# Seven products instead of eight in every second step of a down projection

## The chip, the cores and the metric

The kernel runs on one core of a Trainium2 chip. The metric is the device time of one execution in microseconds: the median of three runs of the kernel before is 1230.73 us (1230.72 to 1230.82). Times inside an execution come from one profiled execution, which took 1231.12 us; its instructions span 1229.3 us of it.

A core has a matrix engine (TensorE, PE in the profile; its weight loads are PEld), a vector engine (VectorE, DVE), a scalar engine (ScalarE, ACT), a third elementwise engine (GpSimd, POOL) and a queue that issues transfers from memory (SyncE, SP). Each takes its instructions strictly in the order written for it and waits where an operand is not ready. Matrix products are written to PSUM, which has eight banks of 128 rows by 512 float32 columns; everything else works from SBUF.

## What is computed

A decoder layer over 272 tokens (16 learned ones and 256 of the input) of width 2048: a normalisation, one input projection, eight retention heads and four mLSTM heads, an output projection, and then a gated MLP of width 5632 with a causal convolution of three taps. Only the 256 input tokens leave. The part that matters here is the last line of the layer and the final normalisation:

```python
up = causal_dwconv(u @ w_up.astype(u.dtype), ffn_conv_w, ffn_conv_b)
gate, val = jnp.split(up, [FFN_DIM], axis=-1)
return h + (jax.nn.silu(gate) * val) @ w_down.astype(h.dtype)
...
h = rmsnorm(h, norm_final)
```

`silu(gate) * val` is a 256 x 5632 matrix, `w_down` is 5632 x 2048; the product of the two is "the down projection".

## The kernel before

**Split operands.** Every float32 operand of a large product is split into two parts of a narrower format that the matrix engine takes at full rate: `hi` is a rounded copy, made by ScalarE (`nc.scalar.copy`), and `lo = x - hi`, made by VectorE (`nc.vector.tensor_tensor` with both inputs in SBUF). A product is three matmuls: hi by hi, lo of the activations by hi of the weights, hi of the activations by lo of the weights. Weights arrive by a transfer of 512 KB (128 x 1024 float32) into a tile `wraw` (4 buffers), are split into `whi` and `wlo` (5 buffers each), and are used once; `load_w` (line 122) does this.

**Stages.** Input projection and heads, output projection, and then the MLP in two halves of 2816 hidden columns each (`for half in range(2)`). A half has an up projection (22 chunks `jj` of 128 hidden columns, gate and value; convolution and silu on VectorE and ScalarE; the result, split, goes to `mh` and `ml`), and a down projection over these 22 chunks. In the profiled execution the two down projections run from 720.5 to 843.7 us and from 1097.8 us to the end.

**The down projection.** For each of four column blocks `b` of 512 columns, two banks `pss` (one per half of the tokens, `tt`) collect the sum over 11 steps `q`. A step takes one weight tile of 2 x 128 hidden rows by 512 columns, and `product` issues six matmuls of 512 columns per token half: 12 a step, 132 a block, 528 a half. After a block, `add` puts the banks onto the residual `hn` (VectorE, one input in PSUM). In the second half `squares` (ScalarE) and `times_gain` (GpSimd) prepare the final normalisation. In the very last block the second token half lags four steps behind the first, so that the first half's normalisation and stores run under the second's products.

**Order.** The program is written straight; the framework that builds it places each instruction on its engine's queue by its own estimate of time, with the order of the text as priority. Tiles with a given number of buffers are reused in turn: the first writer of a new tile waits for the last reader of the tile that had its buffer.

Of the kernel before, what the change touches and what calls it, by code (L numbers as in the profile page):

```python
# [10 lines left out]
F32 = mybir.dt.float32  # L11
# [5 lines left out]
P = 128  # L17
# [66 lines left out]
def trunk(ctx: ExitStack, tc: tile.TileContext, io, out: bass.AP):  # L84
# [75 lines left out]
    def rsqrt_m2(work, v, n, after):  # L160

        r0 = work.tile([P, T], F32, name="r0", bufs=1)
# [3 lines left out]
        t = work.tile([P, T], F32, name="rt", bufs=1)  # L166
# [41 lines left out]
    with pool("sq", 1, side="right") as sqp:  # L208
# [51 lines left out]
        with tc.high_priority():  # L260
# [4 lines left out]
            r = rsqrt_m2(wk, ms[:, :T], T, squared)  # L265
# [119 lines left out]
    def variance(s2, mean):  # L385
# [8 lines left out]
        return rsqrt_m2(wk, var[:, :NQ], NQ, copied)  # L394
# [177 lines left out]
    ssq = up.tile([P, NQ], F32, name="ssq")  # L572

    def out_tile(n, ps):
# [5 lines left out]
        if n == 0:  # L580
            nc.scalar.activation(ssq, h, AF.Square)
        else:
            s2 = wk2.tile([P, NQ], F32, name="s2b")
            sq = nc.scalar.activation(s2, h, AF.Square)
            nc.gpsimd.tensor_tensor(out=ssq, in0=ssq, in1=s2, op=ALU.add)
            return sq
# [11 lines left out]

    mixp_cm.__exit__(None, None, None)

    def norm2():
        ms2 = at.tile([P, 512], F32, name="atps")
        nc.tensor.matmul(ms2[:, :NQ], inv_dm, ssq, start=True, stop=True)
        r = rsqrt_m2(wk2, ms2[:, :NQ], NQ, squared)
# [6 lines left out]
    gfin = midp.tile([P, DM], F32, name="gfin")  # L611
    nc.gpsimd.dma_start(gfin, io["gfin"])
    ss4 = midp.tile([P, 2, 5], F32, name="ss4")
    junk = midp.tile([P, 512], F32, name="junk")
# [65 lines left out]

    NQD = NHF // 2
    for half in range(2):
        mh = midp.tile([P, NHF, SEQ], F32R, name="mh")
        ml = midp.tile([P, NHF, SEQ], F32R, name="ml")
        for jj in range(NHF):
# [10 lines left out]
            copied = nc.scalar.copy(mh[:, jj, :], gt)  # L696
            parted = nc.vector.tensor_tensor(out=ml[:, jj, :], in0=gt, in1=mh[:, jj, :].bitcast(F32), op=ALU.subtract)
# [5 lines left out]

        def product(ps, tt, q, w, first=0, last=NQD - 1, c0=0):

            hi, lo = w
            rows = slice(tt * P, (tt + 1) * P)
            cols = slice(c0, c0 + ps.shape[1])
            for i in range(2):
                k = 2 * q + i  # L710
                nc.tensor.matmul(ps, mh[:, k, rows], hi[:, i, cols], start=k == 2 * first, stop=False)  # L711
                nc.tensor.matmul(ps, ml[:, k, rows], hi[:, i, cols], start=False, stop=False)  # L712
            for i in range(2):
                k = 2 * q + i
                nc.tensor.matmul(ps, mh[:, k, rows], lo[:, i, cols], start=False, stop=k == 2 * last + 1)  # L715
# [5 lines left out]
        if half == 1:  # L721
            wk2_cm.__exit__(None, None, None)
            up_cm.__exit__(None, None, None)
            more_cm = pool("more", 4, side="right")
            more = more_cm.__enter__()
        for b in range(4):
            pss = [at.tile([P, 512], F32, name="atps") for _ in range(2)]
            last = half == 1 and b == 3


            lag = 4 if last else 0
            c = b * 512
            ws = {}
            for q in range(NQD):
                ws[q] = load_w(io["wd"][b, half * NQD + q], [P, 2, 512], more if last and q % 2 else wpool)
                product(pss[0], 0, q, ws[q])
                if q >= lag:
                    product(pss[1], 1, q - lag, ws.pop(q - lag), last=NQD - 1 - lag)
            if not last:
                for tt in range(2):  # L740
                    add(pss[tt], tt, c)
                    if half == 1:
                        squares(tt, b, c, c + 512)
                        times_gain(tt, c, c + 512)
                continue
            add(pss[0], 0, c)
# [3 lines left out]
            add(pss[1], 1, c)  # L750
            for i in range(2):
                ps = at.tile([P, 512], F32, name="atps")[:, 0:256]
                for q in sorted(ws):
                    product(ps, 1, q, ws[q], NQD - lag, c0=i * 256)
                add(ps, 1, c + i * 256)
# [89 lines left out]
```

## Time and profile before

| what | value |
|---|---|
| median of three runs | 1230.73 us |
| the profiled execution | 1231.12 us |
| span of its instructions | 1229.3 us |
| TensorE busy | 1219.7 us, 99% of the span |
| VectorE busy | 841.0 us, 68% |
| ScalarE busy | 655.9 us, 53% |
| GpSimd busy | 53.2 us, 4% |
| weights and inputs read | 222.98 MB, 185 GB/s over the span |

A row of a group has the line of the program, the engine, the operation, the output and the inputs, the shape and the count, and then the busy time of all and the mean of one in ns. A row of a timeline has the start in us, the duration in us, the engine, the line and the operation; "x2" means that two instructions in a row were merged into one row. "Idle before" names what ended a wait. Matmuls overlap in a pipeline, so that what one costs is the distance from its start to the next one's and not its duration.

### The profile page before, as it was taken

What the parts mean: (1) busy time and instruction counts of PE and PEld (TensorE: products, weight loads), DVE (VectorE), ACT (ScalarE), POOL (GpSimd) and SP (SyncE); (2) the same over time, 40 slices, a digit from 0 to 9 for tenths busy, and PEclk for the clock granted to TensorE, in tenths of its full rate; (3) what the DMA queues carried; (4) which work ended last, traced back from release to release, by engine and by line L of the source; (5) the groups of instructions that cost most, each with busy time, mean ns of one, the idle gap of its engine ahead of it and who ended that gap; (6) DMA issues with size and microseconds to landing.
All of it is one profiled execution on the core that took longest, in us unless ns stands there. A gap on an engine that the chain in (4) does not pass through costs nothing.

```text
span 1229.3 us, 22301 instructions
## 1 busy us (share of the span) xinstructions
PE 1219.7 (99%) x9034; PEld 1169.6 (95%) x9034; DVE 841.0 (68%) x1267; ACT 655.9 (53%) x879; POOL 53.2 (4%) x63
## 2 busy tenths in 40 slices
PE   9999999999999999999999999999999999999997
PEld 9999999999999999999999988889999999998886
DVE  8967878767775767787887754445677677664452
ACT  8747656656557556555555543334555555554441
POOL 0100001111100110000000000000000000000000
PEclk9999999999999999999999999999999999999999
DMA  7765565565564656555555665655555556556561
GB/s 275 275 205 159 176 190 172 185 190 175 178 189 143 216 180 216 177 186 187 176 186 188 175 185 189 188 188 189 184 178 188 185 178 187 181 180 188 188 206 69
DMA packets 73287, 228.88 MB, mean 186 GB/s; under 512 B 13408, under 2 KB 17632, under 8 KB 73056
## 3 DMA queue, kind: packets, MB, share of 16 engines
q1 hardware_dynamic: 71952, 223.85, 57.7%
q0 software_dynamic: 656, 2.76, 0.7%
q8 instruction: 70, 1.15, 0.4%
q10 hardware_dynamic: 576, 0.85, 0.2%
q14 instruction: 33, 0.27, 0.1%
HBM read 222.98 MB, written 4.46 MB: 185 GB/s over the span
## 4 chain that ended last, share of the span: by engine, by line
PE 99%; DMA 0%; ACT 0%; DVE 0%; SPq 0%; DVEq 0%; issue 0%; ACTq 0%
PE mmps L137 25%; PE mmps L140 25%; PE mmps L138 25%; PE atps L711 7%; PE atps L712 7%; PE atps L715 7%; PE atps L380 1%; PE atps L372 0%; DMA hT<-in_xT 0%; PE atps L137 0%; PE atps L140 0%; PE atps L381 0%; PE atps L138 0%; PE atps L373 0%; PE atps L382 0%; PE atps L238 0%
## 5 line engine op out<-in xcount | busy, mean ns | idle before, releaser
L128 ACT CAST whi<-wraw 128x1024 fp32r<-128x1024 f32 x404 | 423.2, 1050 | 474.4 <-PE mmps L138 254.8
L130 DVE TENSOR_TENSOR wlo<-wraw,whi 128x1024 fp32r<-128x1024 f32 x404 | 495.8, 1229 | 186.0 <-ACT whi L128 181.0
L138 PE MATMUL mmps<-ul,whi 128*128 128x258 f32 x1408 | 345.8, 283 | 0.0
L137 PE MATMUL mmps<-uh,whi 128*128 128x258 f32 x1408 | 345.5, 282 | 0.0
L137 PEld LDWEIGHTS mmps<-uh,whi 128*128 128x128 f32 x1408 | 266.1, 189 | 0.1
L138 PEld LDWEIGHTS mmps<-ul,whi 128*128 128x128 f32 x1408 | 265.1, 188 | 0.1
L137 PE MATMUL mmps<-xh,whi 128*128 128x272 f32 (+2 forms) x864 | 220.1, 287 | 0.0
L138 PE MATMUL mmps<-xl,whi 128*128 128x272 f32 (+2 forms) x864 | 218.9, 286 | 0.0
L140 PE MATMUL mmps<-uh,wlo 128*128 128x258 f32 x1408 | 198.9, 284 | 0.0
L140 PEld LDWEIGHTS mmps<-uh,wlo 128*128 128x128 f32 x1408 | 182.4, 189 | 0.0
L137 PEld LDWEIGHTS mmps<-xh,whi 128*128 128x128 f32 x864 | 162.8, 188 | 0.1
L138 PEld LDWEIGHTS mmps<-xl,whi 128*128 128x128 f32 x864 | 162.5, 188 | 0.0
L711 PE MATMUL atps<-whi,mh 128*128 128x512 f32 (+1 forms) x360 | 140.5, 391 | 0.0
L712 PE MATMUL atps<-whi,ml 128*128 128x512 f32 (+1 forms) x360 | 140.2, 390 | 0.0
L140 PE MATMUL mmps<-xh,wlo 128*128 128x272 f32 (+2 forms) x864 | 127.1, 286 | 0.0
L140 PEld LDWEIGHTS mmps<-xh,wlo 128*128 128x128 f32 x864 | 114.7, 188 | 0.0
L715 PE MATMUL atps<-wlo,mh 128*128 128x512 f32 (+1 forms) x360 | 110.7, 388 | 0.0
L625 DVE TENSOR_TENSOR cu<-mmps,rstd 128x258 f32<-128x258 f32 x88 | 37.6, 427 | 97.6 <-PE mmps L140 97.1
L711 PEld LDWEIGHTS atps<-whi,mh 128*128 128x128 f32 x360 | 67.6, 188 | 15.8
L715 PEld LDWEIGHTS atps<-wlo,mh 128*128 128x128 f32 x360 | 67.0, 188 | 16.0
L712 PEld LDWEIGHTS atps<-whi,ml 128*128 128x128 f32 x360 | 67.6, 188 | 15.1
L138 PE MATMUL mmps<-mixl,whi 128*128 128x258 f32 x256 | 63.1, 283 | 0.0
(213 smaller groups left out, 1040.3 us busy)
## 6 DMA issues: line engine op xcount, KB each, us to landing
wraw<-in_wu SPq DMA_DIRECT2D x176, 512.0 KB, 3.5
wraw<-in_wi SPq DMA_DIRECT2D x108, 512.0 KB, 4.0
wraw<-in_wd SPq DMA_DIRECT2D x88, 512.0 KB, 3.5
wraw<-in_wo SPq DMA_DIRECT2D x32, 512.0 KB, 3.7
wraw<-in_w SPq DMA_DIRECT2D x7, 320.0 KB, 5.1
hT<-in_xT SPq DMA_DIRECT2D x7, 272.0 KB, 5.5
e<-in_decay POOLq DMA_DIRECT2D x8, 209.0 KB, 3.0
away<-turns SPq DMA_DIRECT2D x4, 288.0 KB, 4.4
```

What stands on the lines that cost most here:

```text
L128: nc.scalar.copy(hi, raw)
L130: nc.vector.tensor_tensor(out=lo, in0=raw, in1=hi.bitcast(F32), op=ALU.subtract)
L137: nc.tensor.matmul(ps, hi[:, k, :], xh(kk), start=kk == first, stop=False)
L138: nc.tensor.matmul(ps, hi[:, k, :], xl(kk), start=False, stop=False)
L140: nc.tensor.matmul(ps, lo[:, k, :], xh(kk), start=False, stop=kk == last)
L380: nc.tensor.matmul(ps[:, 0:NQ], lhs(0), pT[:, 0:CA], start=True, stop=False)
L625: nc.vector.tensor_tensor(out=u, in0=ps[:, :NQ], in1=rstd2, op=ALU.mult)
L711: nc.tensor.matmul(ps, mh[:, k, rows], hi[:, i, cols], start=k == 2 * first, stop=False)
L712: nc.tensor.matmul(ps, ml[:, k, rows], hi[:, i, cols], start=False, stop=False)
L715: nc.tensor.matmul(ps, mh[:, k, rows], lo[:, i, cols], start=False, stop=k == 2 * last + 1)
```

## The change

The 11 steps of a half are divided into six plain ones (q = 0, 2, 4, 6, 8, 10) and five fast ones (1, 3, 5, 7, 9), and two neighbouring column blocks are done at once, so that a step covers 2 token halves x 2 chunks of hidden rows x 2 column blocks. A plain step is what it was, for two weight tiles: 24 matmuls. A fast step takes the 2 x 2 block product by the Strassen-Winograd scheme: seven products of three matmuls, 21 in all, of sums of blocks.

- **Sums of the activations** (four 128 x 128 sums for each pair of chunks, S1 to S4) are made in the up projection by GpSimd in the tile `tb`, and split into `sh` and `sl`, which hold seven operands per fast step in place of four.
- **Sums of the weights** are made in each fast step: the two tiles `raw0` (a `wraw`) and `raw1` (a tile of its own, one buffer) arrive; GpSimd makes four sums of 128 x 512 into `ta` and `tb` (one buffer each), one after the other; then `raw0`, one half of `raw1`, `ta` and `tb` are split by ScalarE and VectorE and multiplied.
- **Banks.** Four banks `cs` collect the four results as before; three of the seven products go straight into them. The other four products collect over the five fast steps in the four banks `ps`, and `share` then distributes them over the four results: a copy on ScalarE and eight additions on VectorE, through the tile `ta`.
- **The end.** In the second half the pair of blocks 2 and 3 does its plain steps for block 2 alone (12 matmuls each); block 3's six plain steps follow behind, with the old lag between the token halves.
- **Room.** To make room, the work tiles of the second normalisation and of the squares move to other tiles, `gfin` (the final gain, 1 MB) is loaded only once the last up projection is over, and the pool `more` of the last block has 3 buffers in place of 4.

```diff
-        mh = midp.tile([P, NHF, SEQ], F32R, name="mh")
-        ml = midp.tile([P, NHF, SEQ], F32R, name="ml")
+        mh = midp.tile([P, 2 * len(PLAIN), SEQ], F32R, name="mh")
+        ml = midp.tile([P, 2 * len(PLAIN), SEQ], F32R, name="ml")
+        sh = midp.tile([P, len(FAST), 7, P], F32R, name="sh")
+        sl = midp.tile([P, len(FAST), 7, P], F32R, name="sl")
...
+                nc.gpsimd.tensor_tensor(out=sums[:, S1, :], in0=a21, in1=a22, op=ALU.add)
+                nc.gpsimd.tensor_tensor(out=sums[:, S3, :], in0=a11, in1=a21, op=ALU.subtract)
+                nc.gpsimd.tensor_tensor(out=sums[:, S2, :], in0=sums[:, S1, :], in1=a11, op=ALU.subtract)
+                nc.gpsimd.tensor_tensor(out=sums[:, S4, :], in0=a12, in1=sums[:, S2, :], op=ALU.subtract)
+                split(sh[:, f, A12:, :], sl[:, f, A12:, :], gt.rearrange("p (a t) -> p a t", a=2))
+                copied, parted = split(sh[:, f, 0:4, :], sl[:, f, 0:4, :], sums)
...
+        def seven(w0, w1, q, cs, ps, fresh):
+
+            f = FAST.index(q)
+            raw0 = wpool.tile([P, 2, 512], F32, name="wraw", bufs=4)
+            nc.sync.dma_start(raw0, w0)
+            raw1 = midp.tile([P, 2, 512], F32, name="raw1")
+            nc.sync.dma_start(raw1, w1)
+
+            ta, tb = (midp.tile([P, 2, 512], F32, name=n) for n in ("ta", "tb"))
+            sums = ((ta, 1, raw1[:, 1, :], raw1[:, 0, :], ALU.subtract), (tb, 0, ta[:, 1, :], raw0[:, 0, :], ALU.add),
+                    (ta, 0, raw1[:, 0, :], raw0[:, 0, :], ALU.subtract), (tb, 1, raw0[:, 1, :], tb[:, 0, :], ALU.subtract))
+            for t, i, a, b, op in sums:
+                nc.gpsimd.tensor_tensor(out=t[:, i, :], in0=a, in1=b, op=op)
+            first, last = q == FAST[0], q == FAST[-1]
+            for w, to in (
+                (raw0, ((A11, ps[0], first, last), (A12, cs[0, 0], False, False))),
+                (raw1, (None, (S4, cs[0, 1], first and fresh, False))),
+                (ta, ((S1, ps[1], first, last), (S3, ps[2], first, last))),
+                (tb, ((S2, ps[3], first, last), (A22, cs[1, 0], False, False))),
+            ):
+                hi = wpool.tile([P, 2, 512], F32R, name="whi", bufs=5)
+                lo = wpool.tile([P, 2, 512], F32R, name="wlo", bufs=5)
+                a = 1 if to[0] is None else 0
+                split(hi[:, a:, :], lo[:, a:, :], w[:, a:, :])
+                for i in range(a, 2):
+                    m, o, begin, _ = to[i]
+                    nc.tensor.matmul(o, sh[:, f, m, :], hi[:, i, :], start=begin, stop=False)
+                    nc.tensor.matmul(o, sl[:, f, m, :], hi[:, i, :], start=False, stop=False)
+                for i in range(a, 2):
+                    m, o, _, end = to[i]
+                    nc.tensor.matmul(o, sh[:, f, m, :], lo[:, i, :], start=False, stop=end)
+
+        def share(ps, b):
+
+            p1, p5, p7, p6 = ps
+            x = midp.tile([P, 2, 512], F32, name="ta")[:, 0, :]
...
+            nc.scalar.copy(x, p1)
+            plus(h(0, 0), p1, h(0, 0))
+            plus(x, p6, x)
+            plus(h(0, 1), p5, h(0, 1))
+            plus(h(0, 1), x, h(0, 1))
+            plus(x, p7, x)
+            plus(h(1, 0), x, h(1, 0))
+            plus(x, p5, x)
+            plus(h(1, 1), x, h(1, 1))
...
-        for b in range(4):
-            pss = [at.tile([P, 512], F32, name="atps") for _ in range(2)]
+        for b in (0, 2):
+            cs = {}
+            for j in range(2):
+                for tt in range(2):
+                    cs[tt, j] = at.tile([P, 512], F32, name="atps")
+            ps = [mm.tile([P, 512], F32, name="mmps") for _ in range(4)]
+
+            final = half == 1 and b == 2
+            for q in range(NQD):
+                if q in FAST:
+                    seven(io["wd"][b, half * NQD + q], io["wd"][b + 1, half * NQD + q], q, cs, ps, final)
+                    if q == FAST[-1]:
+                        share(ps, b)
+                    continue
+                for j in range(1 if final else 2):
+                    w = load_step(b + j, q)
+                    for tt in range(2):
+                        product(cs[tt, j], tt, q, w, q == PLAIN[0], q == PLAIN[-1])
```

**GpSimd's queue.** Before, GpSimd's whole work from the output projection to the end is this (a name's number tells one buffer's tile from the next):

```order
L585 TENSOR_TENSOR ssq<-ssq,s2b 128x258 x14
L612 DMA gfin<-in_gfin 128x2048
L585 TENSOR_TENSOR ssq<-ssq,s2b 128x258
L643 TENSOR_TENSOR hn<-hn,gfin 128x512 x6
L643 TENSOR_TENSOR hn<-hn,gfin 128x256
```

Now, in the second and third fast step of the first half's first pair of blocks:

```order
L757 TENSOR_TENSOR ta_9069<-raw1_9067 128x512
L757 TENSOR_TENSOR ta_9069<-raw1_9067,wraw_9065 128x512
L757 TENSOR_TENSOR tb_9070<-ta_9069,wraw_9065 128x512
L757 TENSOR_TENSOR tb_9070<-wraw_9065,tb_9070 128x512
L757 TENSOR_TENSOR ta_9152<-raw1_9150 128x512
L757 TENSOR_TENSOR ta_9152<-raw1_9150,wraw_9148 128x512
L757 TENSOR_TENSOR tb_9153<-ta_9152,wraw_9148 128x512
L757 TENSOR_TENSOR tb_9153<-wraw_9148,tb_9153 128x512
```

The four sums of a step stand back to back and nothing else stands between two steps: 20 such groups in the program, all with both inputs in SBUF.

**VectorE's queue.** Before, in the first half's down projection, VectorE splits one weight tile per step, eleven a block, and adds two banks at the end of each:

```order
L130 TENSOR_TENSOR wlo<-wraw,whi 128x1024 x11
L719 TENSOR_TENSOR hn<-atps,hn 128x512 x2
L130 TENSOR_TENSOR wlo<-wraw,whi 128x1024 x11
L719 TENSOR_TENSOR hn<-atps,hn 128x512 x2
L130 TENSOR_TENSOR wlo<-wraw,whi 128x1024 x11
```

Now, in two plain and two fast steps of the first half:

```order
L130 TENSOR_TENSOR wlo<-wraw,whi 128x1024 x2
L697 TENSOR_TENSOR wlo<-wraw,whi 128x1024
L697 TENSOR_TENSOR wlo<-raw_9067,whi 128x512
L697 TENSOR_TENSOR wlo<-ta,whi 128x1024
L697 TENSOR_TENSOR wlo<-tb,whi 128x1024
L130 TENSOR_TENSOR wlo<-wraw,whi 128x1024 x2
L697 TENSOR_TENSOR wlo<-wraw,whi 128x1024
L697 TENSOR_TENSOR wlo<-raw_9150,whi 128x512
L697 TENSOR_TENSOR wlo<-ta,whi 128x1024
L697 TENSOR_TENSOR wlo<-tb,whi 128x1024
```

A plain step has two splits as before (for two blocks), a fast step three and a half where it had two. The splits of `ta` and `tb` stand behind GpSimd's sums, and the next step's splits stand behind them.

**The turn from one pair of blocks to the next**, on VectorE, in the first half (`raw_9457` is the second pair's first `raw1`; L784 is `share`, L798 is `add`):

```order
L784 TENSOR_TENSOR hn<-ta,hn 128x512
L798 TENSOR_TENSOR hn<-atps,hn 128x512
L697 TENSOR_TENSOR wlo<-raw_9457,whi 128x512
L784 TENSOR_TENSOR ta<-mmps,ta 128x512
L798 TENSOR_TENSOR hn<-atps,hn 128x512
L784 TENSOR_TENSOR hn<-ta,hn 128x512
L784 TENSOR_TENSOR ta<-mmps,ta 128x512
L798 TENSOR_TENSOR hn<-atps,hn 128x512
L784 TENSOR_TENSOR hn<-ta,hn 128x512
L798 TENSOR_TENSOR hn<-atps,hn 128x512
L697 TENSOR_TENSOR wlo<-ta,whi 128x1024
L697 TENSOR_TENSOR wlo<-tb,whi 128x1024
```

The last `hn<-ta` of `share` stands behind three additions from the banks of the last plain step, and GpSimd's first sum of the next pair writes into the buffer of that `ta`.

102 lines of the change are left out of this document (63 added, 39 removed).

## Prediction

> **What bounds the kernel now.** I read the page's totals and its chain of waits first, then the groups of the down projection, then windows and waits inside it.
>
> ```profile
> span 1229.3 us, 22301 instructions
> PE 1219.7 (99%) x9034; PEld 1169.6 (95%) x9034; DVE 841.0 (68%) x1267; ACT 655.9 (53%) x879; POOL 53.2 (4%) x63
> PE 99%; DMA 0%; ACT 0%; DVE 0%; SPq 0%; DVEq 0%; issue 0%; ACTq 0%
> ...
> L711 PE MATMUL atps<-whi,mh 128*128 128x512 f32 (+1 forms) x360 | 140.5, 391 | 0.0
> L715 PE MATMUL atps<-wlo,mh 128*128 128x512 f32 (+1 forms) x360 | 110.7, 388 | 0.0
> ```
>
> The chain is TensorE for 99% of the span and its groups show 0.0 of idle time before them: a matmul taken away is time gained as long as nothing else becomes late. The room beside TensorE in this stage:
>
> ```profile
> core 0: us, PE busy (x) PEld busy (x) DVE busy (x) ACT busy (x) POOL busy (x), PEclk, DMA share, GB/s
> 720.00:836.00 116.00, 116.00 (x501) 93.45 (x501) 55.87 (x52) 44.61 (x44) 0.00 (x0) 1.00 0.60 187
> 836.00:1104.00 268.00, 268.00 (x2173) 265.27 (x2172) 185.30 (x271) 140.35 (x183) 0.00 (x0) 1.00 0.58 183
> 1104.00:1221.00 117.00, 117.00 (x527) 95.26 (x525) 55.45 (x57) 45.10 (x57) 9.60 (x7) 1.00 0.52 166
> ...
> DVE wlo L130 <- ACT whi L128: 56.8, 37, 1.6
> ACT whi L128 <- PE atps L712: 67.9, 39, 1.8
> ```
>
> In the first down projection VectorE is busy 56 of 116 us and GpSimd not at all. The two waits (from 722 to 834 us) say why: ScalarE waits for TensorE to give a `whi` buffer back and VectorE waits for ScalarE. The splits run five tiles ahead.
>
> **What is removed.** A matmul's cost is the distance between starts:
>
> ```profile
> 720.54 0.39 PE L711 MATMUL atps<-whi,mh 128*128 128x512 f32 x1
> ...
> 843.74 0.28 PE L137 MATMUL mmps<-uh,whi 128*128 128x258 f32 x1
> ```
>
> The first half's 528 matmuls take 843.74 - 720.54 = 123.20 us, 0.2333 us each. There are 2 halves x 2 pairs x 5 = 20 fast steps, each with 21 matmuls for 24: 60 x 0.2333 = **14.0 us** less on the bounding engine.
>
> The Trainium skill (TensorE: Matmul & The Clock Gate, Back-to-back issue gap) gives some 131 ns per matmul of 512 columns in a sustained stream with weight loads. By that figure the gain would be 60 x 0.131 = 7.9 us; the trace has 233 ns in just such a stream, and the sum goes by the trace.
>
> **What is added: a path that GpSimd and VectorE share.** The timeline of the two engines after the second half's first block shows what happens when both run on SBUF:
>
> ```profile
> 1126.61 1.22 DVE L130 TENSOR_TENSOR wlo<-wraw,whi 128x1024 fp32r<-128x1024 f32 x1 [1.58 <-ACT whi L128]
> 1127.75 0.68 DVE L719 TENSOR_TENSOR hn<-atps,hn 128x512 f32<-128x512 f32 x1
> ...
> 1129.40 1.22 DVE L130 TENSOR_TENSOR wlo<-wraw,whi 128x1024 fp32r<-128x1024 f32 x1
> 1130.08 2.95 POOL L643 TENSOR_TENSOR hn<-hn,gfin 128x512 f32<-128x512 f32 x2 [661.68 <-ACT junk L639]
> 1131.74 1.29 POOL L643 TENSOR_TENSOR hn<-hn,gfin 128x512 f32<-128x512 f32 x1
> ...
> 1162.54 1.29 POOL L643 TENSOR_TENSOR hn<-hn,gfin 128x512 f32<-128x512 f32 x1
> 1163.01 1.90 DVE L130 TENSOR_TENSOR wlo<-wraw,whi 128x1024 fp32r<-128x1024 f32 x1 [1.58 <-ACT whi L128]
> ```
>
> GpSimd's 128x512 product takes 1.29 us. The one that began at 1130.08, under a split, took 1131.74 - 1130.08 = 1.66 us, as if it had begun at 1131.74 - 1.29 = 1130.45: 1.05 us after the split began. The split that began at 1163.01, under GpSimd, took 1.90 us for 1.22, as if begun at 1163.69: 1.15 us after GpSimd's 1162.54. Each waits out the other. So I count the two as one server. With a PSUM input VectorE isn't held up; earlier in the program, under GpSimd:
>
> ```profile
> 39.15 4.99 POOL L551 TENSOR_TENSOR rope<-rope,rstd 128x272 f32<-128x272 f32 x4 [37.76 <-DVE rstd L266]
> 40.40 0.42 DVE L468 TENSOR_TENSOR cx<-atps,rstd 128x272 f32<-128x272 f32 x1
> ```
>
> Prices on this server. A split of 128x1024: 1.14 us (1126.61 to 1127.75, start to start) or, before a GpSimd instruction, 1.05; the half split of `raw1` about half, 0.6 or 0.55 (estimate). A weight sum, 128x512 on GpSimd with two SBUF inputs like the rows above: 1.29 or 1.15. A fast step has 3 1/2 splits and 4 sums: 3 x 1.14 + 0.6 + 4 x 1.29 = 9.2 us, or 3 x 1.05 + 0.55 + 4 x 1.15 = 8.3. A plain step has two splits: 2.3 or 2.1. `share` has three additions with both inputs in SBUF, some 0.6 each: 1.8.
>
> *Three of the four pairs of blocks* (six plain, five fast steps): TensorE 6 x 24 x 0.2333 + 5 x 21 x 0.2333 = 33.6 + 24.5 = 58.1 us (61.6 before). The server: 5 x 9.2 + 6 x 2.3 + 1.8 = 61.6, or 5 x 8.3 + 6 x 2.1 + 1.8 = 55.9. TensorE waits 3.5 us a pair or none: 0 to 10.5 us for three.
>
> *The last pair* (second half, blocks 2 and 3): plain steps for one block only, 12 matmuls, so TensorE has 6 x 2.8 + 24.5 = 41.3 us. The server keeps its five fast steps, six single splits and `share`, and has four gains of the blocks before (the order puts them among these sums): 46 + 6.8 + 1.8 + 4 x 1.29 = 59.8, or 41.5 + 6.3 + 1.8 + 4.6 = 54.2. TensorE waits **12.9 to 18.5 us**. The six plain steps of block 3 behind it (16.8 us of matmuls, 6.8 of splits) give nothing back: `ta`, `tb` and `raw1` have one buffer each, so sums run one step ahead at most.
>
> Together 12.9 to 29.0; between the ends I take 21, since sums stand back to back on GpSimd and splits on VectorE, so that both prices occur.
>
> **The turns.** VectorE has eight additions of `share` and four `add` between two pairs:
>
> ```profile
> L719 DVE TENSOR_TENSOR hn<-atps,hn 128x512 f32<-128x512 f32 x8 | 5.5, 688 | 12.1 <-PE atps L715 12.1
> ```
>
> At 0.69 us that is 8.3 us, with the splits of q = 10 and of the next q = 0 and first fast step (4 x 1.14 + 1.7 = 6.3) 14.6, under 11.2 us of matmuls of these two plain steps. Behind them wait the matmuls that need the banks, the split that TensorE needs next, and GpSimd's first sum, whose buffer of `ta` `share` still reads. The excess is 3.4 us and the tiles split ahead cover up to all of it: 0 to 3.4 us at three turns, 0 to 10 in all; I take 2 each, 6.
>
> **What I cost at nothing.** ScalarE's copies (1.05 us each for 5 1/2 tiles in a fast and a plain step, 5.8 us under 10.5). The up projections' four 128-column sums and one longer split per pair of chunks: VectorE is busy 185 of 268 us there; without that room about 1.5 us x 10. The transfers: the same bytes; each `raw1` goes out behind the last reader of the one before, priced with the rivals. `gfin`'s load: its first reader comes a pair later. The lag and stores at the end are as before.
>
> **The sum.** -14.0 + 21 + 6 = **+13 us**: a span of 1242.3 against 1229.3, and as the profiled execution took 1231.12 and the median is 1230.73, a time of 1230.7 + 13 = **1244 us**. By the ends: -14.0 + 12.9 + 0 = -1 and -14.0 + 29.0 + 10 = +25, so 1230 to 1256.
>
> The Trainium skill (SBUF — State Buffer, Who interferes with whom) says that a vector instruction with two SBUF inputs and a GpSimd instruction that reads SBUF exclude one another for the whole instruction. By whole durations (1.22 and 1.29) a fast step would hold the path 9.4 us and the waits be 5.5 x 3 + 20.2 = 37, so +29 with the turns, 1260, the forecast's upper edge; by that rule the trace agrees on the exclusion but not on its length, since the holder lets go 0.14 to 0.17 us early, and I give its length no chance of its own.
>
> **Rivals.**
>
> *The gain is hidden work after all (faster).* If sums and splits overlapped, VectorE alone would need some 34 us of a pair's 58.1 (5 x 4.0 + 6 x 2.3) and only the single buffers would tell:
>
> ```profile
> wraw<-in_wd SPq DMA_DIRECT2D x36, 512.0 KB, 3.5
> ```
>
> A load of `raw1` and four sums are 3.5 + 5.2 = 8.7 us a step, against 10.5 us of matmuls in a plain and a fast step (covered) and 7.7 in the last pair: 5 x 1.0 = 5 us. -14 + 5 + 0 to 6: 1222 to 1228. For it: VectorE's and GpSimd's own totals fit. Against it: the 1.90 and the 1.66 us above. Chance 0.15.
>
> *Even.* The lower prices hold and the turns are covered: the last pair alone eats the gain, -1 to +2 us, 1229.5 to 1233. Chance 0.08.
>
> *Load and sums become one chain (much slower).* If each step's `raw1` goes out only after the step before has done its last sum (it is queued behind a `wraw` that waits for that sum in some places), and each sum first waits out a split, a step lasts 3.5 + 4 x (1.15 + 1.05) = 12.3 us: 1.8 over in 15 steps, 4.6 in 5: 27 + 23 = 50, less 14: +36, 1267. It decides as soon as `raw1` lands after the last split of the step before. Against it: in other places `raw1` stands ahead of the waiting load, and five split tiles give slack. Chance 0.09, some of it below 1259.
>
> My forecast, the shared path with some late turns, has 0.68.
>
> **How the numbers follow.** 0.2%, about what a measurement of this kernel can tell from no change, is 2.5 us. Faster, under 1228.3: 0.15. Same, to 1233.2: 0.08 for "even", less its edge, plus a little of the forecast's: 0.08. Slower: 0.77. The forecast's own range is 1233 to 1256; the range that holds eight in ten, 1227 to 1259, reaches into the faster rival and the chain.
>
> **What would show it.** Splits in fast steps with means well over 1.22 us and weight sums well over 1.29 us; TensorE's idle time ending mostly with ScalarE's copies of `ta` and `tb` and released through them by GpSimd; most of it after the last pair begins, less in the three pairs before; 60 matmuls fewer and their distance still 0.233 us. I am wrong if the sums stay at 1.29 and the splits at 1.22 side by side, or if the last pair takes less than 50 us for its 41.3 of matmuls.

## The result, and the profile after

The changed kernel takes **1246.24 us** (1244.31 to 1246.59) where the kernel before, in the same rounds, takes 1230.78. The ratio is **1.0121, 95% interval 1.0104 to 1.0139**: slower by 15.5 us. The forecast was 1244 us, its range 1227 to 1259.

The page of the changed kernel, in the order of the prediction's rows: totals, the granted clock in 40 slices, and the chain of waits. The last line is the clock of the kernel before.

```profile
span 1244.5 us, 22568 instructions
PE 1217.1 (98%) x8974; PEld 1160.6 (93%) x8974; DVE 943.1 (76%) x1349; ACT 690.1 (55%) x933; POOL 233.6 (19%) x183
PEclk9999999999999999999999999999999999999798
PE 89%; POOL 3%; DVE 3%; DMA 2%; issue 2%; ACT 1%; SPq 0%; DVEq 0%; POOLq 0%; ACTq 0%
...
PEclk9999999999999999999999999999999999999999
```

There are 8974 matmul records for 9034, the 60 that the change removes. TensorE's part of the chain has fallen from 99% to 89%; GpSimd and VectorE have come in, and in two of the last slices the clock is not full; before, every slice has the digit 9, which is 90% or more.

Where the 15.2 us of span lie shows in the windows of the three last stages, cut at the first matmul of each (down projection of the first half, up projection of the second, down projection of the second up to its last matmul). The columns are length, then busy time and count of TensorE, its weight loads, VectorE, ScalarE and GpSimd, granted clock, DMA share and GB/s.

```profile
720.66:845.38 124.72, 119.40 (x500) 92.38 (x499) 96.17 (x82) 60.22 (x67) 66.36 (x36) 1.00 0.52 174
845.38:1099.44 254.06, 254.06 (x2113) 254.06 (x2112) 190.99 (x276) 136.42 (x181) 26.70 (x24) 1.00 0.58 189
1099.44:1236.00 136.56, 124.14 (x524) 97.63 (x522) 104.46 (x100) 65.74 (x84) 72.47 (x44) 0.94 0.45 153
```

The same three windows of the kernel before:

```profile
720.54:843.74 123.20, 123.20 (x531) 99.11 (x530) 60.15 (x56) 46.55 (x47) 0.00 (x0) 1.00 0.60 188
843.74:1097.80 254.06, 254.06 (x2114) 254.06 (x2113) 176.60 (x260) 133.49 (x175) 0.00 (x0) 1.00 0.58 183
1097.80:1221.00 123.20, 123.20 (x554) 100.28 (x552) 59.88 (x64) 49.49 (x62) 9.60 (x7) 1.00 0.52 167
```

The up projection takes 254.06 us in both: the 128-column sums that were added to it cost no time there. A half's down projection has 30 matmuls fewer, 123.20 - 30 x 0.2333 = 116.2 us of matmuls. The first half takes 124.72 and so lost 8.5 us to waits, of which 5.3 stand as idle time of TensorE and the rest as short delays inside rows that count as busy. The second half takes 136.56: 20.4 us lost, of which 12.4 are idle time. 28.9 us are lost in all.

Whom TensorE waited for, and the weight sums and plain splits as groups (busy us, mean ns, idle before):

```profile
PE mmps L771 <- ACT whi L696: 14.5, 9, 4.2
PE atps L740 <- DVE hn L798: 1.2, 2, 0.7
PE mmps L775 <- DVE wlo L697: 0.9, 2, 0.7
```

```profile
L757 POOL TENSOR_TENSOR tb<-wraw,tb 128x512 f32<-128x512 f32 x20 | 40.4, 2022 | 1.3
L757 POOL TENSOR_TENSOR ta<-raw,wraw 128x512 f32<-128x512 f32 x20 | 38.5, 1925 | 0.0
L757 POOL TENSOR_TENSOR ta<-raw 128x512 f32<-128x512 f32 x20 | 33.6, 1680 | 119.0 <-DMA raw<-in_wd 75.0 <-DMA wraw<-in_wu 19.6 <-DVE hn L784 18.0
L757 POOL TENSOR_TENSOR tb<-ta,wraw 128x512 f32<-128x512 f32 x20 | 32.4, 1618 | 10.8 <-DMA wraw<-in_wd 10.8
```

The 80 sums take 1.62 to 2.02 us in the mean, not the 1.26 to 1.29 that one takes alone. Most of the waiting ends with a `whi` copy of ScalarE in a fast step (L696), and ScalarE's copies of `ta` and `tb` in turn waited 34.7 us for GpSimd's `ta` and 40.2 for its `tb`, over the whole program.

The turn into the last pair holds the longest of them. The timeline there, TensorE, then GpSimd, then VectorE (start, duration, idle time before in brackets with its releaser):

```profile
1167.13 0.79 PE L771 MATMUL mmps<-whi,sh 128*128 128x512 f32 x1 [3.22 <-ACT whi L696]
1174.27 0.79 PE L771 MATMUL mmps<-whi,sh 128*128 128x512 f32 x1 [4.21 <-ACT whi L696]
1174.86 0.63 PE L772 MATMUL mmps<-whi,sl 128*128 128x512 f32 x1
1175.28 0.63 PE L771 MATMUL atps<-whi,sh 128*128 128x512 f32 x1
```

```profile
1163.50 1.28 POOL L757 TENSOR_TENSOR ta<-raw 128x512 f32<-128x512 f32 x1 [2.55 <-DVE hn L784]
1164.74 1.27 POOL L757 TENSOR_TENSOR ta<-raw,wraw 128x512 f32<-128x512 f32 x1
1165.96 3.51 POOL L644 TENSOR_TENSOR hn<-hn,gfin 128x512 f32<-128x512 f32 x2
1169.44 1.26 POOL L757 TENSOR_TENSOR tb<-ta,wraw 128x512 f32<-128x512 f32 x1
1170.66 1.26 POOL L644 TENSOR_TENSOR hn<-hn,gfin 128x512 f32<-128x512 f32 x1
1171.88 1.26 POOL L757 TENSOR_TENSOR tb<-wraw,tb 128x512 f32<-128x512 f32 x1
1174.32 2.29 POOL L757 TENSOR_TENSOR ta<-raw,wraw 128x512 f32<-128x512 f32 x1
```

```profile
1174.25 1.23 DVE L697 TENSOR_TENSOR wlo<-tb,whi 128x1024 fp32r<-128x1024 f32 x1 [5.91 <-ACT whi L696]
1175.39 2.31 DVE L130 TENSOR_TENSOR wlo<-wraw,whi 128x1024 fp32r<-128x1024 f32 x1
```

Two things are to be seen. The first sum starts only when `share` (L784) has read `ta` for the last time, and three gains (L644) stand among the four sums of this step, which therefore don't stand back to back as GpSimd's queue above has it for the other steps; VectorE is idle for 5.91 us meanwhile, since the next split in its queue needs a sum. And from 1174.32 on, a sum takes 2.29 us and the split beside it 2.31 us, each nearly twice its own time. The matmuls behind the waits are 0.43 us apart, not 0.233: the granted clock was 0.50 there.

### The profile page after: what moved, and what is told of

The parts are those of the page before. It is cut to its first block, busy times and chain, and to the rows that moved or that the text cites. A ratio compares the mean times of both kernels' runs of the same rounds, so it can differ in the third digit from the quotient of the medians.

```text
span 1244.5 us, 22568 instructions
## 1 busy us (share of the span) xinstructions
PE 1217.1 (98%) x8974; PEld 1160.6 (93%) x8974; DVE 943.1 (76%) x1349; ACT 690.1 (55%) x933; POOL 233.6 (19%) x183
## 4 chain that ended last, share of the span: by engine, by line
PE 89%; POOL 3%; DVE 3%; DMA 2%; issue 2%; ACT 1%; SPq 0%; DVEq 0%; POOLq 0%; ACTq 0%
PE mmps L137 25%; PE mmps L140 25%; PE mmps L138 25%; PE atps L740 2%; PE atps L741 2%; PE atps L743 2%; POOL tb L757 2%; DMA raw<-in_wd 2%; DVE wlo L697 1%; POOL ta L757 1%; PE mmps L771 1%; PE mmps L775 1%; PE mmps L772 1%; PE atps L775 1%; PE atps L772 1%
## 5 line engine op out<-in xcount | busy, mean ns | idle before, releaser
L128 ACT CAST whi<-wraw 128x1024 fp32r<-128x1024 f32 x364 | 380.5, 1050 | 340.9 <-PE mmps L138 249.4
L130 DVE TENSOR_TENSOR wlo<-wraw,whi 128x1024 fp32r<-128x1024 f32 x364 | 461.5, 1271 | 71.1 <-ACT whi L128 66.9
L740 PE MATMUL atps<-whi,mh 128*128 128x512 f32 (+1 forms) x200 | 78.9, 396 | 1.2 <-DVE hn L798 1.2
L741 PE MATMUL atps<-whi,ml 128*128 128x512 f32 (+1 forms) x200 | 78.2, 393 | 0.0
L722 POOL TENSOR_TENSOR tb<-gt 128x128 f32<-128x128 f32 x10 | 14.0, 1403 | 312.0 <-ACT whi L128 282.1
L137 PE MATMUL mmps<-mixh,whi 128*128 128x258 f32 x256 | 62.5, 283 | 0.0
L743 PE MATMUL atps<-wlo,mh 128*128 128x512 f32 (+1 forms) x200 | 59.6, 386 | 0.0
L757 POOL TENSOR_TENSOR ta<-raw 128x512 f32<-128x512 f32 x20 | 33.6, 1680 | 119.0 <-DMA raw<-in_wd 75.0
```

The source lines that it names most:

```text
L128: nc.scalar.copy(hi, raw)
L130: nc.vector.tensor_tensor(out=lo, in0=raw, in1=hi.bitcast(F32), op=ALU.subtract)
L137: nc.tensor.matmul(ps, hi[:, k, :], xh(kk), start=kk == first, stop=False)
L740: nc.tensor.matmul(ps, mh[:, k + i, rows], hi[:, i, cols], start=first and i == 0, stop=False)
L741: nc.tensor.matmul(ps, ml[:, k + i, rows], hi[:, i, cols], start=False, stop=False)
L743: nc.tensor.matmul(ps, mh[:, k + i, rows], lo[:, i, cols], start=False, stop=last and i == 1)
```

## The experiments

"Shared path" is the prediction's theory: an instruction of GpSimd and one of VectorE that both read SBUF take turns. "Turn" is the work between two pairs (`share`, `add`, gains), behind which the sums stand. "Chain" is load and sums one behind the other. Ratios are to the kernel before, 1230.7 to 1231.3 us, run in between.

**The four weight sums on VectorE.** GpSimd then reads SBUF in the down projection for the gains alone.

```diff
             for t, i, a, b, op in sums:
-                nc.gpsimd.tensor_tensor(out=t[:, i, :], in0=a, in1=b, op=op)
+                nc.vector.tensor_tensor(out=t[:, i, :], in0=a, in1=b, op=op)
```

> The changed kernel with the four weight sums of each fast step on VectorE in place of GpSimd; nothing is left out. Shared path (my forecast's theory): a sum costs the path 0.6 us on VectorE in place of 1.15 to 1.29 on GpSimd, a fast step 4.0 + 2.4 = 6.4 us in place of 9.2. In three pairs 5 x 6.4 + 13.8 + 8.3 of share and add = 54 us fit under 58.1 of matmuls: no waits there; the last pair needs 32 + 6.8 + 8.3 + 4.8 of gains = 52 against 41.3: some 10 us of waits stay, with VectorE busy throughout. Time 1230 us (1224 to 1234). Rival, one chain of load and sums through single buffers: the chain shrinks to 3.5 + 2.4 = 5.9 us a step, under the 7.7 of the last pair, so all waits but the turns go: 1217 to 1222. Rival, waits come from the turns alone: 1246 less nothing.

Measured: 1236.77 us, ratio 1.0047 (1.003 to 1.0064), 9.5 us faster than the change. VectorE takes 0.69 to 0.74 us for a sum where GpSimd took 1.62 to 2.02. Neither rival's time fits (1217 to 1222 for the chain, 1246 for the turns). The time is also 2.8 us above the shared path's band, which was unexplained at this point. In the profile TensorE still waits 4.24 us at the turn into the last pair, where GpSimd's gains stretch three of VectorE's sums to 1.4 to 1.8 us.

**Sums that read almost nothing.** The weight sums stay on GpSimd, but each adds 16 columns and fills the other 496 by two writes that read nothing; the rest of the sums is left out of the computation.

```diff
             for t, i, a, b, op in sums:
-                nc.gpsimd.tensor_tensor(out=t[:, i, :], in0=a, in1=b, op=op)
+                nc.gpsimd.tensor_tensor(out=t[:, i, 0:16], in0=a[:, 0:16], in1=b[:, 0:16], op=op)
+                for _ in range(2):
+                    nc.gpsimd.memset(t[:, i, 16:], 0.5)
```

> The changed kernel with each weight sum on GpSimd replaced by a sum of 16 of its 512 columns and two fills of the other 496, which read nothing; the other columns of the sums are left out of the result. The order of loads, sums and splits, their buffers and waits stay, and so, about, does GpSimd's time per sum when undisturbed (1.2 to 1.4 us); what goes is that GpSimd reads SBUF while VectorE splits. Shared path: splits go back to 1.22 us, GpSimd's four steps to some 5 us, and the time to 1222 to 1228. Rival, chain of load and sums and late turns, with the sharing a side effect: 1240 or more.

Measured: **1225.0 us, ratio 0.995 (0.9935 to 0.9965)**, 21 us less than the change. The waits of TensorE in this run, and the splits between 1152 and 1200 us, where GpSimd fills and adds beside them:

```profile
PE mmps L773 <- ACT whi L696: 5.6, 1, 5.6
```

```profile
L130 DVE TENSOR_TENSOR wlo<-wraw,whi 128x1024 fp32r<-128x1024 f32 x10 | 12.1, 1224 | 1.1 <-ACT whi L128 1.1
L697 DVE TENSOR_TENSOR wlo<-wraw,whi 128x1024 fp32r<-128x1024 f32 x4 | 4.9, 1228 | 0.1
```

GpSimd is as busy as with an undisturbed sum (0.39 to 0.47 us for the 16 columns and twice 0.51 for the writes, in the mean), the loads and buffers are the same, and the splits are back at 1.22 us. So the doubled times come from the reads. One reservation: the writes don't need the load and stand partly ahead of it, so that the way from a load to its last sum is shorter too; how much of the 21 us that is, this run does not say. The Trainium skill (SBUF — State Buffer, Who interferes with whom) has this distinction: VectorE with two SBUF inputs contends with a GpSimd instruction that reads SBUF and not with one that only writes it. The trace agrees: the splits take 1.22 us in a stretch in which GpSimd mostly writes, and 2.31 beside a sum that reads. One wait is left, 5.6 us at the turn into the last pair, where the sums still stand behind `share` and the gains.

**The gains of the last pair, later in the text.** The calls that multiply blocks 0 and 1 by `gfin` were moved behind the last fast step.

```diff
+        late = []
...
-                        times_gain(tt, c, c + 512)
+                        late.append((tt, c))
+            if final:
+                for tt, c in late:
+                    times_gain(tt, c, c + 512)
```

> The changed kernel with the four gains of column blocks 0 and 1 on GpSimd put behind the last fast step of the second half, where they stood between its first sums; nothing is left out. Shared path: 5 us of work leave the last pair and run under block 3's plain steps, and the two long waits of TensorE at its start (3.2 and 4.2 us, after which its clock is at half for some 20 matmuls, 4 us) get shorter: 5 to 9 us less, 1237 to 1241. If the gains only moved waits about: 1246.

Measured: 1246.98 us, ratio 1.0127 (1.0112 to 1.0142). The framework put GpSimd's instructions in the same order as in the change, gains among the sums; the place in the text did not decide it. So this run says nothing of the turn and is a second measurement of the change. The next run ties the gains by an order edge.

**The gains behind the last sum** (`done` is the last fast step's last sum):

```diff
-                        times_gain(tt, c, c + 512)
+                        gains.append((tt, c))
+            if final:
+                with tc.issue_after(done.ins):
+                    for tt, c in gains:
+                        times_gain(tt, c, c + 512)
```

> The change with the four gain products of blocks 0 and 1 tied behind the last weight sum on GpSimd, so that in GpSimd's queue they stand behind all sums of the last pair and not between the first ones. If the waits of 3.2 and 4.2 us at the turn into the last pair, and the half clock behind them, come from these four gains between the sums (4 x 1.27 us of GpSimd and as much held VectorE, then about 3.9 us of slow TensorE): 1237 to 1241 us. If the turn (share's nine instructions, then the sums) makes the waits and the gains only stand in them: 1244 to 1248 us, as the change.

Measured: 1244.04 us, ratio 1.0102 (1.0087 to 1.0117). The theory that the gains' place makes the waits falls: 2.2 us less than the change, where 5 to 9 were expected, and inside the band of the other theory. At the turn the two waits went from 3.22 and 4.21 to 2.96 and 0.99 us, but at the last fast step TensorE waited longer, 1.41 and 1.82 us where it had waited 0.93 and 1.47. There the first sum of GpSimd, the first of these waits, GpSimd's gains, and the clock:

```profile
1202.19 1.29 POOL L757 TENSOR_TENSOR ta<-raw 128x512 f32<-128x512 f32 x1 [5.02 <-DMA raw<-in_wd]
1206.73 0.49 PE L771 MATMUL mmps<-whi,sh 128*128 128x512 f32 x1 [1.41 <-ACT whi L696]
1208.58 6.71 POOL L644 TENSOR_TENSOR hn<-hn,gfin 128x512 f32<-128x512 f32 x3
```

```profile
1210.00:1215.00 5.00, 5.00 (x12) 3.87 (x13) 5.00 (x4) 4.06 (x5) 5.00 (x3) 0.50 0.44 139
```

The sums of this step wait 5.02 us for the load of `raw1`, and TensorE's wait of 1.41 us, for the copy of a sum, is over before the gains begin. The wait of 1.82 us, which ends at 1209.75, is for a split that ran beside the last sum. So the gains made neither. They then take 6.71 us for three instead of 3 x 1.27, and VectorE's splits are held for as long, but TensorE, at half its clock, waits no more. Why the waits of the last step grew is not shown by this run.

**Sums on VectorE and gains late together.** Here `gfin` is loaded behind the loads of the last fast step, so that the gains can't begin before.

```diff
-            nc.gpsimd.dma_start(gfin, io["gfin"])
...
-            nc.sync.dma_start(raw1, w1)
+            loaded = nc.sync.dma_start(raw1, w1)
...
-                        times_gain(tt, c, c + 512)
+                        gains.append((tt, c))
+            if final:
+                with tc.issue_after(done.ins):
+                    nc.sync.dma_start(gfin, io["gfin"])
+                for tt, c in gains:
+                    times_gain(tt, c, c + 512)
```

Here `done` is the last `loaded`.

> Weight sums on VectorE as in the run with the sums on VectorE (1236.8 us), and gfin loaded behind the loads of the last fast step, so that the gains on GpSimd can't start at the turn into the last pair. If the gains are what stretches VectorE's sums there (1.41 to 1.76 us for 0.69): the wait of 4.2 us shrinks to 1 to 2 us and the half clock behind it goes, 1231 to 1234 us. If VectorE's own work at the turn (share 6.2 us and four sums 2.8 us ahead of the first splits) makes the wait: 1236 to 1237.5 us.

Measured: 1239.35 us, ratio 1.0066 (1.0051 to 1.0081), slower than with the sums on VectorE alone; both expectations missed. The wait at the turn did shrink, from 4.24 to 1.94 us, as the first theory has it, but nine others of 0.4 to 1.8 us follow in the last pair. The two longest, 1.82 and 1.70 us, fall beside or just behind the gains, which now run from 1195.19 on, but six come before them. Something else held VectorE too.

**Fast steps in the first half alone**, sums on VectorE:

```diff
-    FAST = list(range(1, NQD, 2))
-    PLAIN = list(range(0, NQD, 2))
+    STEPS = list(range(1, NQD, 2)), []
...
     for half in range(2):
+        FAST = STEPS[half]
+        PLAIN = [q for q in range(NQD) if q not in FAST]
```

> Weight sums on VectorE, fast steps only in the first half (10 of 20), the second half all plain. By the ledger of stages of the run with the sums on VectorE (first half's down projection 120.2 us where it was 123.2, second half +7.5 us): 1227 to 1229 us, faster than before by 0.2%. If the fast steps' loss in the second half is spread over what surrounds them (norm, gains, tail) and not in the fast steps: 1230 to 1234 us.

Measured: 1229.51 us (1227.16 to 1230.65), ratio 0.9987 (0.9977 to 0.9996), between the two bands. The profile decides: the second half's matmuls run from 1096.12 to 1219.3, 123.2 us as before the change, so its loss came with its fast steps. The first half takes 121.5 us and so keeps only 1.7 of the 7.0 that its matmuls gain.

**Two fast steps a pair in the second half**, sums on VectorE, gains late:

```diff
-    STEPS = list(range(1, NQD, 2)), []
+    STEPS = list(range(1, NQD, 2)), [3, 7]
```

> Weight sums on VectorE, gains late, all five fast steps a pair in the first half, two a pair (steps 3 and 7) in the second. If the last pair's waits come from VectorE's work in each fast step (7.9 us for 7.7 us of matmuls, so a run of fast steps has no slack, while two among nine plain steps have it): first half -3.0, third pair -1.4, last pair -1.4 to 0: 1224 to 1227 us. If the turn into the last pair costs what it costs however few fast steps follow: 1228 to 1232 us.

Measured: 1225.73 us (1224.44 to 1229.38), ratio 0.9951 (0.9935 to 0.9968), as the first theory expected: between plain steps these steps fit. The second half has no wait left in the profile. The first half, where nothing differs from the run before this one, shows what had held VectorE. VectorE's timeline, and TensorE's waits (the profile is of the execution of 1229.38 us, the slowest of the four):

```profile
766.03 0.69 DVE L764 TENSOR_TENSOR ta<-raw 128x512 f32<-128x512 f32 x1 [4.39 <-DMA raw<-in_wd]
766.64 0.69 DVE L764 TENSOR_TENSOR ta<-raw,wraw 128x512 f32<-128x512 f32 x1
767.24 1.22 DVE L130 TENSOR_TENSOR wlo<-wraw,whi 128x1024 fp32r<-128x1024 f32 x1
768.37 0.69 DVE L764 TENSOR_TENSOR tb<-ta,wraw 128x512 f32<-128x512 f32 x1
768.98 1.22 DVE L130 TENSOR_TENSOR wlo<-wraw,whi 128x1024 fp32r<-128x1024 f32 x1
```

```profile
PE atps L750 <- DVE wlo L130: 2.7, 2, 2.2
```

Sums of the next fast step stand in VectorE's queue *ahead* of the two plain splits that TensorE needs first. They wait 4.39 us for the load of `raw1`, and the splits behind them wait too, though their data is there: ScalarE's copies for them were done by 761.82. With the sums on GpSimd, VectorE had other work during such a wait: in the changed kernel GpSimd waits 5.00 us for `raw1` up to 1186.08, and VectorE does a plain split at 1183.81.

**The sums behind the split of their own `raw0`**, everything else as in the last run:

```diff
-            for t, i, a, b, op in sums:
-                nc.vector.tensor_tensor(out=t[:, i, :], in0=a, in1=b, op=op)
...
+                _, parted = split(hi[:, a:, :], lo[:, a:, :], w[:, a:, :])
+                if w is raw0:
+                    with tc.issue_after(parted.ins):
+                        for t, j, x, y, op in sums:
+                            nc.vector.tensor_tensor(out=t[:, j, :], in0=x, in1=y, op=op)
```

> As the run with two fast steps a pair in the second half, and in VectorE's queue each fast step's four sums tied behind the split of its own raw0, where they stood ahead of the splits of the plain step before. If the sums, waiting for the load of raw1 (VectorE idle for 4.39 us, TensorE then 2.17 us, in the first half of that run), hold the plain splits behind them: the first half's down projection falls from 120 to 124 us to 117 to 119 us and the time is 1221 to 1224 us. If the late load is what counts, wherever the sums stand: 1225 to 1227 us.

Measured: **1221.38 us** (1221.15 to 1221.69), ratio 0.9918 (0.9903 to 0.9933), as expected of the queue. 120 us of the first half, of the run with the sums ahead and then of this one:

```profile
720.00:840.00 120.00, 116.13 (x485) 90.24 (x484) 94.26 (x113) 57.84 (x64) 0.00 (x0) 0.99 0.52 171
```

```profile
720.00:840.00 120.00, 120.00 (x531) 97.01 (x530) 104.93 (x124) 62.80 (x69) 0.00 (x0) 1.00 0.60 191
```

TensorE has no idle time left with VectorE at 104.93 of 120 us. By matmuls alone the span would be 1229.3 - 14 x 3 x 0.2333 = 1219.5; it is 1219.7.

**Three, four and five fast steps a pair in the second half**, on this order (four are 1, 3, 6 and 8; with five, the lists are the change's own):

```diff
-    STEPS = list(range(1, NQD, 2)), [3, 7]
+    STEPS = list(range(1, NQD, 2)), [2, 5, 8]
```

> As the run with the sums behind the split, with three fast steps a pair (2, 5 and 8) in the second half. If VectorE has room for three among eight plain steps: 1.4 us less than with two, 1220 to 1223 us. If the third fills it in the last pair: the same or more, 1222 to 1227 us.

> As the run with three fast steps a pair in the second half, with four (1, 3, 6 and 8). With room on VectorE: 1.4 us less, 1218.5 to 1220 us. If VectorE fills in the last pair: 1220 to 1223 us.

> All five fast steps a pair in both halves, as in the change (60 matmuls fewer), with the sums on VectorE behind the split of their raw0 and the gains late. If the sums' place in VectorE's queue and the gains made the waits of the runs with sums on VectorE: two fast steps a pair more than in the run with three, 2.8 us less, 1217 to 1219 us. If VectorE's own work fills the last pair (7.9 us for 7.7 us of matmuls in each step, and the share and the norm beside it): 1219 to 1225 us.

Measured: three **1220.56 us, ratio 0.991 (0.9894 to 0.9927)**; four 1224.95, ratio 0.9946 (0.993 to 0.9963); five 1229.48, ratio 0.9986 (0.9976 to 0.9995). Three fit and give the lowest time found: 10.8 us under the kernel before, 25.7 under the change, and 0.8 under the run with two, whose interval overlaps. Its chain:

```profile
PE 97%; DVE 1%; issue 0%; DMA 0%; ACT 0%; SPq 0%; DVEq 0%; ACTq 0%
```

With four and five the expectation of room falls, and both came out above even the other band (1223 and 1225 at most). The last pair of the run with five shows the shared path again, GpSimd, VectorE, and windows behind them:

```profile
1186.89 7.07 POOL L644 TENSOR_TENSOR hn<-hn,gfin 128x512 f32<-128x512 f32 x4 [112.60 <-DMA gfin<-in_gfin]
```

```profile
1187.65 1.79 DVE L770 TENSOR_TENSOR ta<-raw 128x512 f32<-128x512 f32 x1
1192.74 1.77 DVE L770 TENSOR_TENSOR tb<-ta,wraw 128x512 f32<-128x512 f32 x1
```

```profile
1190.00:1195.00 5.00, 2.05 (x8) 1.05 (x6) 5.00 (x4) 1.99 (x2) 3.96 (x3) 0.99 0.00 0
1195.00:1200.00 5.00, 3.84 (x8) 2.64 (x9) 5.00 (x7) 3.73 (x5) 0.00 (x0) 0.50 0.47 147
```

The four gains that are left on GpSimd hold four of VectorE's half-size instructions for about 1.1 us each (1.75 to 1.79 for 0.69) in a pair in which TensorE has waited at each fast step before; TensorE waits 2.25 and 1.40 us and the clock halves behind that. With three fast steps the same gains are hidden. With four, TensorE's only waits in the last pair (0.39, 2.46 and 0.95 us) come beside or just behind such gains. With five, waits of 1.35, 0.48, 0.92 and 0.92 us come before the gains begin, three of them in steps in which VectorE is idle for 1.19 us, since the next split in its queue needs a copy by ScalarE. So of the 9 us between three and five steps the gains make a part only; how large a part was not separated.

**Sums on GpSimd, two fast steps a pair in the second half**, gains behind the last sum as above:

```diff
-    FAST = list(range(1, NQD, 2))
+    STEPS = list(range(1, NQD, 2)), [3, 7]
```

> The change's weight sums on GpSimd, gains behind the last sum, two fast steps a pair (3 and 7) in the second half. The first half is that of the change (124.7 us, 1.5 over before). If the shared path has room where fast steps stand among plain ones, the second half gains its 2.8 us: 1228 to 1231 us. If sums on GpSimd hold VectorE for too long even there (a fast step 9 us of both engines in turn): 1233 to 1238 us.

Measured: 1230.31 us (1228.95 to 1232.22), ratio 0.9992 (0.9983 to 1.0001), as the shared path with room expects. The second half is without waits even with GpSimd's sums; what is lost lies in the first, which takes 124.6 us. Against the run with the sums behind the split on VectorE, 1221.38, whose second half has no waits either, the sums on GpSimd cost 9 us.

## Why the prediction was right

The side, the size and the mechanism held; the terms inside the sum did not all.

**The matmuls.** 60 fewer, and 0.2333 us each where nothing waits: in the run with 14 fast steps in all, the span came out within 0.2 us of what 42 matmuls fewer give. The term of -14.0 us stands.

**The shared path.** That the two engines take turns is shown by the durations: a sum and a split side by side take 2.29 and 2.31 us, and without GpSimd's reads the splits take 1.22. Taking the reads out saves 21 us, but the shorter way from load to last sum is included in these, so that the path's own price in time is not shown alone. The prediction's marks are in the trace too: sums at 1.62 to 2.02 us, splits beside them at 2.3. The rival of hidden work falls by these rows, "even" by the time.

The long chain of load and sums falls by its time, 1267, but not altogether as a mechanism. The prediction's sign for it was that `raw1` lands after the last split of the step before. In the last pair GpSimd's first sums start at 1186.08 and 1205.74, at the end of waits of 5.00 and 4.98 us for the load, and the last splits of the steps before were over at 1183.89 and 1203.59. So in two of its steps the load stood in the chain ahead of TensorE's waits, beside the shared path.

The price on the path held: in the last pair, 1158 to 1217 us, VectorE's splits (21 of 1.22 and 4 of 0.69 us), three of `share`'s additions (0.69) and GpSimd's 24 instructions (1.27) come to 25.6 + 2.8 + 2.1 + 30.5 = 61 us of single durations in 59 us of time. At least one of the two engines is at such work in 55.5 of these 59 us: one server, nearly full, though at times one engine waits for the other's result or for a load and not for the path. Its length was foreseen as 54 to 60.

**The distribution of the waits** was the weak step. The prediction had 21 us of waits from the path in the run of the steps and 6 from the turns. Of the 28.9 us lost, 8.2 stand in the turn into the last pair (0.49, 0.30, 3.22, 4.21) and 3.5 in that of the first half (0.67, 0.70, 0.60, 1.49), together nearly twice the 6; the third pair has none at all. About 12 are spread over the steps, idle time and short delays together, just below the 12.9 that the prediction gave as the least. That five tiles of slack, and a shared path that lets go early, carried the three long pairs nearly through is the likely reason; no run tests it. The prediction named the first sum's wait for `share` at the turns, but added up the excess of `share` and `add` on VectorE alone; it did not follow what the sums need there: four sums in a row behind `share`'s last read of `ta`, VectorE being idle for 3.00 and 2.25 us in the first half's turn and 2.89 and 5.91 in the last.

**The clock.** The prediction had no term for it. In the changed kernel about 5 us (9 x 0.19 + 9 x 0.233 + 5 x 0.233) are lost to matmuls at a reduced clock: between 1167 and 1175 nine of them stand 0.43 us apart, and the next windows of 5 us hold 14 and later 18 where 23 fit.

```profile
1175.00:1180.00 5.00, 5.00 (x14) 3.83 (x13) 5.00 (x4) 2.67 (x4) 4.92 (x3) 0.50 0.42 152
1180.00:1185.00 5.00, 5.00 (x23) 4.03 (x22) 5.00 (x5) 2.95 (x3) 1.07 (x1) 0.99 0.61 224
1215.00:1220.00 5.00, 5.00 (x18) 3.96 (x17) 5.00 (x7) 2.80 (x5) 0.00 (x0) 0.74 0.90 269
```

So 21 + 6 became about 12 + 12 + 5, and the time fell within 2.2 us of the forecast partly by luck, because one term that was too large and two that were too small came out even.

**Costed at nothing.** The up projection's sums: shown (254.06 both times). The tail: 1244.5 - 1236.0 = 8.5 us behind the last matmul, 1229.3 - 1221.0 = 8.3 before. The loads were not free: in the change two of them stood in the chain of the last pair, as said above, and the run with the sums on VectorE ahead of the splits turns the same late load into a wait. No gain waited for `gfin`'s load in the change; its four gains were hidden with two and three fast steps a pair in the second half, and not with more.

**Left open.** Whether a buffer of its own for `share`'s sum (so that the first sums needn't wait for it) removes the turns' 11.7 us is not known: the tiles of the MLP would need 73.16 KB of each row of SBUF with it, and 73.06 are left. How the lost time divides between the shared path and the chain of load and sums was not separated.

## What to carry to other kernels

Before giving work to an idle engine, ask what it reads: an idle GpSimd whose operands lie in SBUF takes its time from VectorE's two-input instructions, and the same sum took 0.69 us on VectorE where it took 1.6 to 2.0 on GpSimd and held a split for as long. When work goes into the queue of a busy engine, place it behind what is due first: sums that waited for a load in front of ready splits cost 4.4 us with two fast steps a pair in the second half and 9.9 with five (1239.35 to 1229.48). And use a cheaper algorithm only as densely as the helper engines, with all else they have to do there, allow: three fast steps a pair in the second half gave 10.8 us, five gave 1.7.

## What the runs showed of the hardware that was not expected

**The clock halves after short waits.** After a wait of 3.22 us the matmuls stand 0.43 us apart. In the run with fast steps in the first half alone a single wait of 1.78 us was enough:

```profile
767.27 1.73 PE L750 MATMUL atps<-wlo,mh 128*128 128x512 f32 x4 [1.78 <-DVE wlo L130]
768.79 0.63 PE L747 MATMUL atps<-whi,mh 128*128 128x512 f32 x1
769.22 0.63 PE L748 MATMUL atps<-whi,ml 128*128 128x512 f32 x1
```

Yet one wait of 1.94 us (sums on VectorE, late gains) left the clock at 1.00, and 2.25 and 1.40 us within 5 us (five fast steps) brought it to 0.50. So the length of a wait alone does not decide. In all traces the stretches at half clock before the last matmul last 3.41 us or a multiple of it (6.83, 13.65). Counted back in steps of 3.41 us from a later drop in the same run (1205.28), a boundary falls at 1160.91, in the middle of the wait of 1.94 us (1160.00 to 1161.94). That fits a clock that is set anew every 3.41 us by how idle TensorE was in the 3.41 us before. With all traces cut up in this way, stretches at full clock with 1.98 us or more of idle time were all followed by half the clock, those with 1.48 or less never, and those between by either. This is an inference from the times; no run was made to test it.

The Trainium skill (TensorE: Matmul & The Clock Gate, What's actually happening) puts the drop behind an idle window of about 3.4 us; the traces agree on the size of the drop and on the 3.4 us, and show that such a window need not be idle throughout. At the turn into the last pair 7.4 us of waits cost 3.8 us more in this way: nine matmuls 0.19 us apart too far, and nine fewer in the window behind.

**Two instructions that start side by side on the shared path both show nearly the sum of their times**: 2.29 and 2.31 us for a pair of 1.27 and 1.22. Their busy time in the profile contains the waiting, so VectorE's 96 us in the first half's window are not 96 us of work.
